# Running the stages of three token jobs at the same time in a four-layer decoder trunk on eight cores

## Chip, cores, metric

One Trainium2 chip, all 8 cores, one sequence of the prompt and 16 sample sequences on each; no core talks to another. The metric is the time of one execution in device microseconds, that of the slowest core. Executions come in two states: fast, and slow, where one die (cores 0 to 3 or 4 to 7) shows a lower granted TensorE clock and the time is some per cent longer. The kernel before took 3514 to 3523 us in the undisturbed runs of every round of experiments, so times of different rounds can be set side by side.

In the profile's lines PE is TensorE's matmuls, PEld its weight loads, DVE VectorE, ACT ScalarE and POOL GpSimd. SBUF is where the kernels keep their tiles, PSUM where their matmuls put their sums (the tile PS in the lines). A table load is an ACT_TABLE_LOAD in ACT's list: 289 of them in the trace of the kernel before, 1283 ns each.

## The reference, cut to what matters

Four layers. On a core each handles 2048 prompt tokens and 16 x 4 sample tokens, 2112 in all, with 1024 channels.

```python
h = layer_norm(x) * (1 + scale) + shift                # per-sequence modulation from c
a_x, a_z, b_cg, b_bg, b_x, b_z, g_a, g_b = split(h @ w_in)   # 8 x 1024 columns
# branch A: conv4 -> gates r, i (block diagonal) -> a = exp(c r ..), b = sqrt(1-a^2) i x -> scan over tokens
o_a = (scan(a, b) * silu(a_z)) @ w_a_out
# branch B: conv3 of (b_cg * b_x), gated
o_b = (b_bg * conv3 * silu(b_z)) @ w_b_out
out = (sigmoid(g_a) * o_a + sigmoid(g_b) * o_b) @ w_o
x   = layer_norm(ALPHA * x + gate * out) * ln_g + ln_b
```

Data is channel by token: 8 chunks of 128 channels on the partitions, tokens along the free dimension. Phase 1 is everything up to the two branch products, phase 2 the two output projections with their sigmoid gates, phase 3 `w_o` with the residual.

## The kernel before: the parts that matter

The 2048 tokens go in two passes of 1024, each through all four layers with X resident in SBUF, in tiles of 512; the 64 sample tokens ride along in the first pass as a thin third tile. A greedy scheduler orders each engine's list ahead of time, and the program has each list in that order, with the semaphores to wait for.

```python
def tiles_of(s):
    if s == 0:
        return [(0, 0, 512, "p"), (1, 512, 512, "p"), (2, 1024, 64, "s")]
    return [(0, 0, 512, "p"), (1, 512, 512, "p")]
...
for s in range(2):
    load_x(s)                                  # TensorE transposes
    ...
    for (n, c0, W, kind) in tiles_of(s):
        ln_in(0, n, c0, W, kind)
    for l in range(DEPTH):
        phase1(l, s)
        for gi, g in enumerate(groups_of(s)):  # two groups of tiles
            phase2(l, s, g, gi)
            phase3(l, s, g, gi)                # ends with ln_out(l) and ln_in(l + 1)
```

```python
# LayerNorm statistics: two ones-matmuls per chunk, 16 a tile
cp("dve", xr, X[:, c, c0:c0 + W], ...)
P.add("pe", lambda e, ...: e.matmul(ps1, ones, xr, start=(c == 0), stop=(c == NCH - 1)), ...)
act(sq, X[:, c, c0:c0 + W], AF.Square, ...)
P.add("pe", lambda e, ...: e.matmul(ps2, ones, sq, ...), ...)
...
act(TZ, az, AF.Tanh, ..., scale=0.5)                      # SiLU as tanh and a product
stt(TZ, TZ, 1.0, az, ALU.add, ALU.mult, ...)
...
act(A2, A2, AF.Sqrt, ..., bias=0.25, scale=-0.25)         # in phase 1, stage 2
```

Of the kernel before, what the change touches and what calls it, by code (L numbers as in the profile page):

```python
# [7 lines left out]
BF16 = mybir.dt.bfloat16  # L8
AF = mybir.ActivationFunctionType
ALU = mybir.AluOpType  # L10

D = 1024
# [5 lines left out]
ST = 4  # L18
ALPHA = (2.0 * DEPTH) ** 0.25
LN_EPS = 1e-6  # L20
UNITS_PER_LAYER = 45
TW = 1088

STAT_FP32R = True
CFG = dict(tslots=4, mulalt=True, groupwise=True, nwb=8, single_bx=False, ln_dedicated=False, lnr=4, window=100)

class Buf:
    __slots__ = ("name", "w", "rs", "const")

    def __init__(self, name):  # L30
        self.name = name
        self.w = None
        self.rs = []
        self.const = False

class Op:
    __slots__ = ("eng", "fn", "deps", "sem", "val", "inc", "cost", "lat", "tbl", "idx", "start", "finish", "dma")

ENGS = ("pe", "act", "dve", "pool", "sp")
SYNC_LAT = 0.25  # L40
TBL_SWITCH = 1.3
WINDOW = 48
SCHEDULE = True
PRIO_Q = 0.4

class Prog:
# [10 lines left out]
    def add(self, eng, fn, reads=(), writes=(), dma=None, cost=0.3, lat=0.0, tbl=0):  # L57
        deps = []
        for b in reads:
            if b.w is not None:  # L60
                deps.append(b.w)
        for b in writes:
            if b.w is not None:
                deps.append(b.w)
            deps.extend(b.rs)
        op = Op()
        op.eng = eng
        op.fn = fn
        op.cost = cost
        op.lat = lat  # L70
        op.tbl = tbl
        op.idx = self.nops
        self.nops += 1
        op.dma = dma
        op.start = None
        op.finish = None
        if dma is None:
            op.sem = self.esem[eng]
            op.val = None
            op.inc = 1  # L80
        else:
            if dma not in self.dsem:
                self.dsem[dma] = self.stack.enter_context(self.nc.semaphore("dsem_" + dma))
                self.dcnt[dma] = 0
            self.dcnt[dma] += 16
            op.sem = self.dsem[dma]
            op.val = self.dcnt[dma]
            op.inc = 16
        seen = set()
        dl = []  # L90
        for d in deps:
            if id(d) not in seen and d is not op:
                seen.add(id(d))
                dl.append(d)
        op.deps = dl
        for b in reads:
            if not b.const:
                b.rs.append(op)
        for b in writes:
            b.w = op  # L100
            b.rs = []
        self.q[eng].append(op)
        return op

    def schedule(self):
        pend = {e: list(self.q[e]) for e in ENGS}
        allops = sorted((o for e in ENGS for o in self.q[e]), key=lambda o: o.idx)
        bl = {}
        succ_max = {}
        for o in reversed(allops):  # L110
            b_ = o.cost + o.lat + succ_max.get(id(o), 0.0)
            bl[id(o)] = b_
            for d in o.deps:
                v = b_ + (0.0 if d.eng == o.eng else SYNC_LAT)
                if succ_max.get(id(d), 0.0) < v:
                    succ_max[id(d)] = v
        head = {e: 0 for e in ENGS}
        free = {e: 0.0 for e in ENGS}
        newq = {e: [] for e in ENGS}
        cur_tbl = 0  # L120
        remaining = sum(len(v) for v in pend.values())
        done = {e: [False] * len(pend[e]) for e in ENGS}
        while remaining:
            best = None
            for e in ENGS:
                lst = pend[e]
                n = len(lst)
                h = head[e]
                while h < n and done[e][h]:
                    h += 1  # L130
                head[e] = h
                cnt = 0
                i = h
                cand = None
                while i < n and cnt < CFG['window']:
                    if not done[e][i]:
                        cnt += 1
                        op = lst[i]
                        rdy = 0.0
                        ok = True  # L140
                        for d in op.deps:
                            if d.finish is None:
                                ok = False
                                break
                            t = d.finish if d.eng == e and d.dma is None else d.finish + SYNC_LAT
                            if t > rdy:
                                rdy = t
                        if ok:
                            st = rdy if rdy > free[e] else free[e]
                            sw = 1 if (e == "act" and op.tbl != 0 and op.tbl != cur_tbl) else 0  # L150
                            key = (round((st + (TBL_SWITCH if sw else 0.0)) / PRIO_Q), -bl[id(op)], op.idx)
                            if cand is None or key < cand[0]:
                                cand = (key, st, sw, i, op)
                    i += 1
                if cand is not None and (best is None or cand[0] < best[1][0]):
                    best = (e, cand)
            assert best is not None, "scheduler deadlock"
            e, (key, st, sw, i, op) = best
            if sw:
                st += TBL_SWITCH  # L160
                cur_tbl = op.tbl
            elif e == "act" and op.tbl != 0:
                cur_tbl = op.tbl
            op.start = st
            free[e] = st + op.cost
            op.finish = st + op.cost + op.lat
            done[e][i] = True
            newq[e].append(op)
            remaining -= 1
# [3 lines left out]
    def emit(self):  # L173
        nc = self.nc
        prog = self
# [7 lines left out]
        def run(ename, eng):  # L183
            waited = {}
            for op in prog.q[ename]:
                for d in op.deps:
                    if ename == "pe" and d.eng == "pe" and d.dma is None:
                        continue
# [4 lines left out]
                ins = op.fn(eng)  # L193
                ins.then_inc(op.sem, op.inc)
            if ename == "sp":
                for op in prog.finals:
# [5 lines left out]
        with nc.Block() as block:  # L202
# [19 lines left out]

def bc_last(ap, n):
    return bass.AP(ap.tensor, ap.offset, [list(x) for x in ap.ap] + [[0, n]])

# [5 lines left out]

def _build(nc, stack):
# [5 lines left out]
    xp_d = dram("xp", [SEQ, D], "ExternalInput")  # L238
    xs_d = dram("xs", [NSB * ST, D], "ExternalInput")
    sst_d = dram("sst", [DEPTH, 96, D], "ExternalInput")  # L240
    cvec_d = dram("cvec", [17, D], "ExternalInput")
    prm_d = dram("prm", [64, D], "ExternalInput")
    wmain_d = dram("wmain", [DEPTH * UNITS_PER_LAYER, 128, 2048], "ExternalInput")
    wc_d = dram("wc", [DEPTH * 12, 128, 2048], "ExternalInput")
    ident_d = dram("ident", [128, 128], "ExternalInput")
    yp_d = dram("yp", [SEQ, D], "ExternalOutput")
    ys_d = dram("ys", [NSB * ST, D], "ExternalOutput")
    pst_d = dram("psto", [DEPTH, 6, D], "ExternalOutput")
    sso_d = dram("sso", [DEPTH, 96, D], "ExternalOutput")
# [3 lines left out]

    X = sb("X", [128, NCH, TW])
    HN = sb("HN", [128, NCH, TW], BF16)
    YA = sb("YA", [128, NCH, TW], BF16)
    YB = sb("YB", [128, NCH, TW], BF16)
    MGW = 576 if CFG["groupwise"] else TW
    MG = sb("MG", [128, NCH, MGW], BF16)
    XB = [[Buf(f"X{c}_{n}") for n in range(3)] for c in range(NCH)]  # L260
    HNB = [[Buf(f"HN{c}_{n}") for n in range(3)] for c in range(NCH)]
    YAB = [[Buf(f"YA{c}_{n}") for n in range(3)] for c in range(NCH)]
    YBB = [[Buf(f"YB{c}_{n}") for n in range(3)] for c in range(NCH)]
    MGB = [[Buf(f"MG{c}_{n}") for n in range(3)] for c in range(NCH)]

    NWB = CFG['nwb']
    WB = [sb(f"WB{i}", [128, 2048], BF16) for i in range(NWB)]
    WBB = [Buf(f"WB{i}") for i in range(NWB)]
    WG = sb("WG", [128, 2048], BF16)
    WGB = Buf("WG")  # L270

    PRM = sb("PRM", [128, NCH, 64])
    PRMB = Buf("PRM")
    SST = sb("SST", [128, DEPTH, NCH, 96])
    SSTB = [[Buf(f"SST{l}_{c}") for c in range(NCH)] for l in range(DEPTH)]
    PST = sb("PST", [128, DEPTH, NCH, 6])
    PSTB = [[Buf(f"PST{l}_{c}") for c in range(NCH)] for l in range(DEPTH)]
    MOD = sb("MOD", [128, DEPTH, 24, 17])
    MODB = [Buf(f"MOD{l}") for l in range(DEPTH)]
    SCT = sb("SCT", [128, NCH, 17])  # L280
    SCTB = Buf("SCT")
    SH = sb("SH", [128, DEPTH, NCH])
    S1 = sb("S1", [128, DEPTH, NCH])
    HBR = sb("HBR", [128, DEPTH, NCH])
    HBI = sb("HBI", [128, DEPTH, NCH])
# [78 lines left out]
    for g_ in isgate:  # L364
        ngidx.append(cnt_)
        if not g_:
            cnt_ += 1
# [671 lines left out]
```

## Time and profile before

| | before |
|---|---|
| median of its first three runs | 3523 us (3516 to 3716, the highest one slow) |
| profiled run, cores | 3502 to 3531 us, granted clock 0.931 to 0.947 |
| TensorE busy | 86% of the span, but 72% by column count (worked out in the prediction) |
| DVE, ACT, POOL busy | 63%, 58%, 39% |
| 16 DMA engines, weight queue | 51.3% |

The way to read it: a matmul's recorded duration overlaps the next one's (512 columns: 379 ns recorded, 216 ns from start to start, medians of the trace), so the busy share of TensorE flatters it.

### The profile page before, as it was taken

The page shows a single profiled execution, that of the slowest core. Times are in us where ns is not written, and L with a number is a line of the kernel's source. Part 1 is how long each engine was busy: PE and PEld are TensorE (multiplying, and loading weights), DVE is VectorE, ACT ScalarE, POOL GpSimd, SP SyncE. Part 2 cuts the span into 40 slices and gives each one's busy share as a digit, 9 for nine tenths or more (in the row PEclk, how much of TensorE's full clock was granted, in tenths as well). Part 3 has the DMA queues.
Part 4 walks back from the last instruction along what each step waited for, and adds up shares of the span by engine and source line. Part 5 has one row for each costly group of instructions (what it writes and reads, how often), then busy time and mean ns, then how long its engine had stood idle before and what let it go on. Part 6 is the DMA issues. An engine that isn't in the chain of part 4 may idle for free.

```text
span 3531.2 us, 56621 instructions; the slowest of 8 cores (3502.1 to 3531.2 us)
## 1 busy us (share of the span) xinstructions
PE 3050.5 (86%) x15904; PEld 1455.2 (41%) x15904; DVE 2238.0 (63%) x3596; ACT 2048.9 (58%) x3386; POOL 1360.4 (39%) x1982
## 2 busy tenths in 40 slices
PE   5698997999978899788888698979999799979987
PEld 3344443444434444433445343434344344434444
DVE  1777457774567756577644587467846785568644
ACT  2677346774447754377633587348834784468623
POOL 1455223553225542245511265225532464235511
PEclk8899998998989999899998799999999899989998
DMA  7455943547544466523566334853387237724573
GB/s 151 66 90 90 142 73 61 88 80 122 89 72 76 79 109 104 95 37 55 83 122 120 88 65 81 134 96 60 67 143 120 42 67 121 131 48 72 93 131 87
DMA packets 88051, 322.39 MB, mean 91 GB/s; under 512 B 9817, under 2 KB 9945, under 8 KB 87746
## 3 DMA queue, kind: packets, MB, share of 16 engines
q0 software_dynamic: 81792, 297.83, 51.3%
q1 hardware_dynamic: 5954, 20.95, 1.8%
q8 instruction: 136, 2.23, 0.2%
q14 instruction: 169, 1.38, 0.1%
HBM read 606.21 MB, written 10.32 MB: 175 GB/s over the span
## 4 chain that ended last, share of the span: by engine, by line
PE 55%; ACT 13%; DVE 11%; issue 10%; POOL 6%; DMA 4%; DVEq 0%; ACTq 0%; POOLq 0%; SPq 0%
PE PS L455 50%; ACT TMPALL L417 9%; DVE TMPALL L441 4%; DVE TMPALL L430 4%; ACT L417 3%; POOL TMPALL L430 3%; PE PS L569 2%; PE PS L572 2%; DMA TMPALL<-xp 1%; DMA WB<-wmain 1%; DVE TMPALL L809 1%; POOL YA L430 1%; PE PS L461 1%; POOL PST L448 1%; POOL YB L430 1%
## 5 line engine op out<-in xcount | busy, mean ns | idle before, releaser
L455 PE MATMUL PS<-HN,WB 128*128 128x512 bf16 (+1 forms) x10240 | 1993.9, 350 | 232.3 <-ACT TMPALL L417 76.6
L455 PEld LDWEIGHTS PS<-HN,WB 128*128 128x128 bf16 x10240 | 866.8, 99 | 1255.8 <-issue 411.6
L417 ACT ACTIVATE TMPALL<-PS 128x512 f32<-128x512 f32 (+1 forms) x1052 | 530.3, 524 | 584.5 <-PE PS L455 433.3
L441 DVE SCALAR_TENSOR_TENSOR TMPALL<-TMPALL,PRM 128x512 f32<-128x512 f32 (+1 forms) x800 | 605.5, 767 | 141.9 <-ACT TMPALL L417 112.7
L441 DVE SCALAR_TENSOR_TENSOR TMPALL<-TMPALL,PS 128x512 f32<-128x512 f32 (+1 forms) x640 | 373.9, 588 | 487.4 <-PE PS L455 406.5
L383 POOL DMA_DIRECT2D WB<-wmain x512 | 288.0, 563 | 1019.2 <-PE PS L455 783.5
L430 POOL TENSOR_TENSOR TMPALL<-TMPALL 128x512 f32<-128x512 f32 (+1 forms) x288 | 380.0, 1328 | 516.9 <-ACT TMPALL L417 425.9
L417 ACT ACT_TABLE_LOAD x289 | 370.8, 1283 | 82.3 <-PE PS L455 28.0
L417 ACT ACTIVATE LNR<-X 128x512 fp32r<-128x512 f32 (+1 forms) x320 | 171.2, 551 | 333.1 <-PE PS L572 208.0
L417 ACT ACTIVATE TMPALL<-TMPALL,PRM 128x512 f32<-128x512 f32 (+1 forms) x320 | 219.2, 692 | 153.3 <-DVE TMPALL L430 103.4
L455 PE MATMUL PS<-MG,WB 128*128 128x512 bf16 (+1 forms) x1280 | 250.5, 353 | 51.8 <-DVE MG L430 27.3
L809 DVE TENSOR_TENSOR_SCAN TMPALL<-TMPALL,PST 128x512 f32<-128x512 f32 x128 | 205.0, 1604 | 88.7 <-POOL TMPALL L430 82.1
L455 PE MATMUL PS<-YA,WB 128*128 128x512 bf16 (+1 forms) x1280 | 259.6, 348 | 1.1 <-ACT TMPALL L417 1.1
L455 PE MATMUL PS<-YB,WB 128*128 128x512 bf16 (+1 forms) x1280 | 255.9, 345 | 2.0 <-DVE TMPALL L441 1.7
L430 DVE TENSOR_TENSOR TMPALL<-X,TMPALL 128x512 f32<-128x512 f32 (+1 forms) x320 | 221.8, 730 | 26.6 <-ACT TMPALL L417 22.7
L430 POOL TENSOR_TENSOR YB<-TMPALL 128x512 bf16<-128x512 f32 x160 | 201.9, 1262 | 80.0 <-DVE TMPALL L430 49.8
L430 POOL TENSOR_TENSOR YA<-TMPALL 128x512 bf16<-128x512 f32 (+1 forms) x160 | 197.2, 1233 | 74.5 <-DVE TMPALL L809 53.9
L430 DVE TENSOR_TENSOR TMPALL<-PS,TMPALL 128x512 f32<-128x512 f32 (+1 forms) x320 | 188.1, 591 | 53.0 <-PE PS L455 22.5
L448 POOL COPY PST<-TMPALL 128x3 f32<-128x3 f32 (+2 forms) x384 | 139.6, 366 | 182.3 <-ACT TMPALL L417 95.9
L455 PEld LDWEIGHTS PS<-MG,WB 128*128 128x128 bf16 x1280 | 109.3, 103 | 183.3 <-issue 84.8
L430 DVE TENSOR_TENSOR TMPALL<-TMPALL 128x512 f32<-128x512 f32 (+2 forms) x224 | 157.4, 727 | 43.1 <-ACT TMPALL L417 32.7
L569 PE MATMUL PS<-LNR,ONES 128*128 128x512 f32 (+1 forms) x320 | 140.8, 474 | 47.7 <-DVE LNR L448 46.2
(69 smaller groups left out, 2563.1 us busy)
## 6 DMA issues: line engine op xcount, KB each, us to landing
WB<-wmain POOLq DMA_DIRECT2D x512, 512.0 KB, 6.9
WB<-wc POOLq DMA_DIRECT2D x48, 512.0 KB, 9.9
TMPALL<-xp SPq DMA_DIRECT2D x16, 512.0 KB, 8.2
yp<-TMPALL SPq DMA_DIRECT2D x16, 512.0 KB
WG<-wmain POOLq DMA_DIRECT2D x8, 512.0 KB, 11.6
TMPALL<-sst SPq DMA_DIRECT2D x4, 384.0 KB, 4.2
sso<-TMPALL SPq DMA_DIRECT2D x4, 384.0 KB
TMPALL<-xs SPq DMA_DIRECT2D x1, 256.0 KB, 11.5
```

Of the source, the lines that this page charges most:

```text
L383: P.add("pool", lambda e, dst=dst, srcd=srcd: e.dma_start(out=dst[:, :], in_=srcd), writes=[dB], dma=tag, cost=0.65, lat=5.0)
L417: return P.add("act", lambda e: e.activation(out=out, in_=in_, func=func, **kw), reads, writes, cost=cost, tbl=TBL.get(func, 0))
L430: return P.add(eng, lambda e: e.tensor_tensor(out=out, in0=in0, in1=in1, op=op), reads, writes, cost=ew_cost(eng, out, True))
L441: return P.add("dve", lambda e: e.scalar_tensor_tensor(out=out, in0=in0, scalar=scalar, in1=in1, op0=op0, op1=op1), reads, writes, cost=ew ...
L448: return P.add(eng, lambda e: e.tensor_copy(out=out, in_=in_), reads, writes, cost=ew_cost(eng, out, False))
L455: ins = e.matmul(out, l_, r_, start=(i == 0), stop=(i == n - 1))
L461: return P.add("pe", lambda e: e.transpose(out, in_, ident), reads, writes, cost=0.12, lat=0.15)
L569: P.add("pe", lambda e, c=c, xr=xr: e.matmul(ps1, ones, xr, start=(c == 0), stop=(c == NCH - 1)), reads=[LNRB[qx], ONESB], writes=[BANKB[b ...
L572: P.add("pe", lambda e, c=c, sq=sq: e.matmul(ps2, ones, sq, start=(c == 0), stop=(c == NCH - 1)), reads=[LNRB[qs], ONESB], writes=[BANKB[b ...
L809: P.add("dve", lambda e: e.tensor_tensor_scan(out=HS, data0=A, data1=TI, initial=PST[:, l, c, 0:1], op0=ALU.mult, op1=ALU.add), [TMPB[qA], ...
```

## The change

The intent is to keep TensorE supplied at every moment, by running stages of different token groups at once. The 2112 tokens become three equal jobs of 704. In slot k, phase 1 of job k, phases 2 and 3 of job k-1, LayerNorm out of job k-2 and LayerNorm in of job k+1 are laid over one another; X lives in DRAM between uses. With it: SiLU as one ACT function, the square root as Ln and Exp, LayerNorm sums pre-added on DVE and POOL, PSUM pairs given out by the scheduler, and the host lays data out channel-major, so no transposes.

```diff
+NJOB = 3
+W = (SEQ + NSMP) // NJOB          # 704
+HW = W // 2                       # a matmul's columns, 352
+NSLOT = DEPTH * NJOB
+P23_FROM, P23_SPAN = 0.01, 0.73
 ... (cut)
-    for s in range(2):
-        load_x(s)
 ... (cut)
-        for l in range(DEPTH):
-            phase1(l, s)
-            for gi, g in enumerate(groups_of(s)):
-                phase2(l, s, g, gi)
-                phase3(l, s, g, gi)
+    for k in range(NSLOT + 2):
+        if k < NSLOT:
+            place(k, p1_events(k))
+        if 1 <= k <= NSLOT:
+            place(k, p23_events(k - 1))
 ... (cut)
+        if 2 <= k:
+            place(k, ln_out_events(k - 2, 0.01, 0.2))
+            if k + 1 < NSLOT:
+                place(k, ln_in_events(k + 1, 0.22, 0.3))
+        if 1 <= k <= NSLOT:
+            place(k, [(0.53, lambda k=k, c=c: fetch_x(k - 1, c), None) for c in range(NCH)])
 ... (cut)
-        act(TZ, az, AF.Tanh, [BANKB[ids[1]]], [TMPB[qTZ]], scale=0.5)
-        stt(TZ, TZ, 1.0, az, ALU.add, ALU.mult, ...)
+                act(halves(T(z)), ps(blk), AF.Silu, [blk], [TMPB[z]], psum=True)
-        act(A2, A2, AF.Sqrt, [TMPB[qA2]], [TMPB[qA2]], bias=0.25, scale=-0.25)
+                act(T(m), T(m), AF.Ln, [TMPB[m]], [TMPB[m]], bias=0.25, scale=-0.25)
+                act(T(m), T(m), AF.Exp, [TMPB[m]], [TMPB[m]], scale=0.5)
```

## The prediction

> **What bounds the kernel now.** I read the table of cores first (3502 to 3531 us, granted clock 0.931 to 0.947, dies alike: a fast run), then the page's busy shares and 40 slices, then the stretches by engine, then who waited for whom.
>
> ```profile
> PE 3050.5 (86%) x15904; PEld 1455.2 (41%) x15904; DVE 2238.0 (63%) x3596; ACT 2048.9 (58%) x3386; POOL 1360.4 (39%) x1982
> PE   5698997999978899788888698979999799979987
> PEclk8899998998989999899998799999999899989998
> ```
>
> TensorE is busiest, but 86% is not its load. The reference fixes that: per layer 512 weight blocks of 128x128 for the input projection, 16 for the gates and 3 x 64 for the three output projections, 720 blocks, each against 2112 tokens on a core, in 4 layers: 6.08 million columns. The spacing of matmuls I take from dense stretches:
>
> ```profile
> core 3: us, PE busy (x) PEld busy (x) DVE busy (x) ACT busy (x) POOL busy (x), PEclk, DMA share, GB/s
> 2030.00:2075.00 45.00, 45.00 (x210) 20.43 (x209) 40.62 (x45) 39.59 (x57) 29.19 (x38) 1.00 0.41 70
> 2957.00:3002.00 45.00, 45.00 (x210) 20.43 (x209) 13.77 (x20) 11.80 (x18) 9.07 (x15) 1.00 0.96 157
> 2207.00:2251.00 44.00, 42.26 (x197) 19.00 (x195) 13.66 (x21) 7.89 (x14) 7.73 (x14) 1.00 1.02 168
> ```
>
> 45 us / 210 = 214.3 ns per 512 columns, 1 ns over 512 columns at 2.4 GHz, so the load is 6.08 million / 2.4 GHz = 2534 us plus 1 ns a matmul: 72% of 3523 us. Some 990 us are lost. The first row is what the reader should keep: in the projection stage (phase 1) all five engines overlap, DVE at 90% and ACT at 88%, and TensorE still runs gapless; in the output stage (rows two and three) the vector engines idle and the DMA queues are full. Where the 990 us go:
>
> ```profile
> 44.00:132.00 88.00, 62.55 (x280) 37.31 (x280) 42.91 (x100) 39.35 (x77) 20.87 (x20) 0.66 0.56 99
> 530.00:618.00 88.00, 62.42 (x372) 32.27 (x371) 66.27 (x159) 59.84 (x117) 31.10 (x39) 0.81 0.37 61
> 1898.00:2030.00 132.00, 90.41 (x474) 54.42 (x472) 78.34 (x149) 68.85 (x119) 30.66 (x36) 0.75 0.44 101
> 2030.00:2207.00 177.00, 164.31 (x753) 72.74 (x752) 147.03 (x163) 143.61 (x205) 107.15 (x140) 1.00 0.43 73
> 132.00:397.00 265.00, 232.48 (x1425) 109.75 (x1424) 188.07 (x348) 191.78 (x345) 136.98 (x237) 0.99 0.56 87
> ```
>
> Here TensorE looks 70% busy in the prologue, at a layer boundary (LayerNorm out, then in, then the next layer) and between the two passes, at clocks of 0.66 to 0.81. Counting only bf16 columns by shape, slice by slice, TensorE does 0 to 25% of its possible work in the prologue (112 of 132 us lost), and 31 to 62 us are lost at each layer boundary, about 114 between the passes and 63 at the end: together some 580 us. The other 400 are thin: phase 1 of the first pass (last row), which drags 64-column tiles along, does about 0.81 of its possible columns; the second pass (fourth row) 753 x 214.3 / 177 us = 0.91.
>
> ```profile
> PE PS L455 <- ACT TMPALL L417: 92.5, 89, 6.9
> PE PS L455 <- DVE TMPALL L441: 66.4, 68, 3.3
> PE PS L455 <- ACT HN L417: 62.3, 5, 17.2
> PE PS L569 <- DVE LNR L448: 46.2, 37, 6.8
> PE PS L455 <- DMA WB<-wmain: 15.3, 7, 2.8
> ```
>
> These are TensorE's own waits: for PSUM to be read, for the LayerNorm chain (third and fourth), hardly for weights. So it is a latency problem at boundaries, not an engine at its limit.
>
> [...] all eight cores show 1.00 in most dense stretches for over 100 us, while core 3 alone has 0.81 from 775 to 925 us. [...] the conv step on 128x512 takes 0.74 us alone and up to 1.47 us, mean 1.07 in the fourth row's stretch. [...] the trace has 289 loads of 1283 ns.
>
> **The change part by part.** It is a rewrite: three jobs of 704 tokens (prompt and samples in one row), in 13 pipeline slots; slot k runs phase 1 of job k, phases 2 and 3 of job k-1, and the LayerNorms of job k-2 and k+1 at once. X lives in DRAM between uses.
>
> TensorE. 720 x 2 halves x 12 = 17280 matmuls of 352 columns: 146.7 + 1 to 2 ns = 148 ns, 2557 us. Weight loads don't bind: 64-column matmuls follow each other at some 30 to 45 ns, with a load each. LayerNorm sums now add on DVE and POOL first, so 16 statistics matmuls per 512-token tile become 4 per 704, 96 in all, about 25 us; modulation 768 tiny ones, about 25. All input and output transposes go (the host does the layout). About 2610 us at full clock, or 217 us per full slot (phase 1: 800 x 148 ns = 118; phases 2 and 3: 640 x 148 ns = 95; 4 for the rest). No time is removed here; the load stays.
>
> DVE per slot, scaling rows of the by-form groups to 704 columns with the 64- and 512-column durations (a PSUM product takes 219 ns at 64 and 684 at 512, 1.04 ns a column, so 0.88 us at 704; the LayerNorm subtraction 217 and 858, so 1.13). Phase 1: the fourth row gives 147/16 = 9.2 us per chunk of 512; Silu on ACT removes two operations of 0.68; times 1.36 for length: 10.7 us x 8 chunks = 85 us. Phases 2 and 3: (2 x 0.88 + 1.0 + 0.95) x 8 = 30. Two LayerNorms: 2 x (1.0 + 1.13 + 1.39) x 8 = 56. Samples about 8. Sum 179 us, 79% of a 227-us slot; the first row above shows 90% harmless.
>
> ACT: 18 operations per chunk (12 in phase 1, two gate Tanh, two squares, two normalising) of 0.76 (from PSUM: 216 ns at 64, 593 at 512) to 0.97 us (with scale and bias by partition) = 14.9, x 8 = 119; some 28 table loads (2 to 3 per chunk, sqrt now as Ln and Exp) x 1.28 = 36; statistics 8: 163 us, 72%. POOL: 5.5 tensor operations of 1.85, copies 2.8, weight issues 3.4 = 16 per chunk, x 8 = 130, 57%.
>
> DMA. 528 + 48 + 4 weight units against 568. The queue needed 51.3% x 3531 / 568 = 3.2 us each: 1850 us; X traffic of 78 MB at the 330 GB/s of the hardware queue (20.95 MB in 1.8% of the span) is 236 more: 2090 us, 73%, spread evenly. A unit serves 32 x 148 ns = 4.7 us of matmuls.
>
> Sum. Prologue about 55 us (8 modulation units 26 us beside X at 9, statistics, then 8 x 2.5 us of normalising) for 132. Slot 0 has phase 1 only and ACT is its limit: about 145. Slots 1 to 11: I choose a fill of 0.955, above the 0.91 of phase 1, since independent output blocks can fill its holes, below the gapless rows: 217 / 0.955 = 227, x 11 = 2499. Last phases 2 and 3: 100. Last LayerNorm and store: 32. Together 2831 us; 1% for spells of 0.81 on the slowest core (150 us at 0.81 costs 28 us): **2850 us**, 19% off.
>
> **The rivals.** (1) The clock limiter. [...] For it: core 3's spell, and one run of before in three at 3716 us. Against: 2030 to 2207 us has all engines loaded at 1.00. Fully throttled: 2610 / 0.81 + 250 = about 3470; a third of the time: 3040. (2) The in-order queues of DVE and ACT become the bound: 79% and 72% on average, with contention if POOL at 57% overlaps DVE more, and only four PSUM pairs. If the DVE's SBUF operations go as in their worst spells, 179 becomes about 220 us a slot and 11 slots take some 2650: 3000 in all. [...] (3) The single X buffer: LayerNorm out, LayerNorm in, reload, phase 3 run in series in each slot; their planned shares (0.20, 0.30, 0.08, 0.14) leave a quarter of a slot free; if DVE lags, slots stretch to 240: 2980. (4) DMA sets the pace: it needs 73%, and 1.02 was reached without TensorE waiting; I expect nothing.
>
> **Range and chances.** A perfect fill gives 11 x 217 + 332 = 2720; fill of 0.90 with some throttling 3050. Range 2710 to 3050. For a gain under 2% a slot would have to take 285 us, above every rival but full throttling. Faster 0.95, same 0.03, slower 0.02.
>
> **What would show it.** Right: bf16 columns at 0.93 to 0.98 of possible from about 200 us to 2650; no slices of low PEclk but at the ends; DVE near 75% of the span, ACT 65 to 70%, DMA over 65%; TensorE's waits for LayerNorm outputs gone. Wrong: a clock near 0.81 in mid-kernel (rival 1); TensorE waiting on ACT or DVE for PSUM for more than 15 us a slot (2); waits of phase 3 for X (3); waits for weights (4). A prologue over 80 us would make that term wrong.

## The result, and the profile after

The changed kernel takes 2866 us (median of 13 runs, 2846 to 3169), the kernel before 3563 us in the 15 runs made by then. The ratio of the fast runs is 0.811 (95% interval 0.809 to 0.814). Ratios here and below are the mean time of one kernel's fast runs over that of the other's of the same rounds, so not quite the ratio of the medians quoted. The profiled run, slowest core 2845 us:

```profile
PE 2658.9 (93%) x18144; PEld 1729.4 (61%) x18144; DVE 2091.2 (74%) x2329; ACT 1716.1 (60%) x2051; POOL 1495.1 (53%) x1818
PE   2889999999999999999999999999999999999995
PEclk9999999999999999999999999999999999999997
q0 software_dynamic: 83520, 304.12, 64.2%
q1 hardware_dynamic: 32688, 81.45, 8.9%
```

The row of 40 slices has no hole between the third and the last: the dips at layer boundaries are gone, and with them the low clock (0.985 on average against 0.94). DMA stands at 64.2 + 8.9 = 73%.

The same stretches as in the prediction's sum, cut where the gate matmuls and the phase 3 matmuls show that a slot begins and ends (columns: stretch, its length, busy time and count of each engine, clock, DMA share, GB/s):

```profile
211.00:2708.00 2497.00, 2421.15 (x16439) 1578.16 (x16437) 1855.27 (x2064) 1538.40 (x1833) 1343.74 (x1654) 0.99 0.74 136
62.00:211.00 149.00, 128.43 (x927) 81.02 (x928) 122.86 (x107) 106.61 (x128) 106.30 (x105) 0.97 0.83 150
0.00:62.00 62.00, 5.80 (x132) 4.85 (x132) 36.08 (x51) 22.32 (x34) 20.33 (x32) 1.00 0.99 194
2708.00:2815.00 107.00, 101.37 (x643) 64.41 (x644) 56.19 (x80) 35.09 (x43) 21.37 (x26) 0.95 0.59 123
```

From the top: slots 1 to 11, slot 0, the prologue, the last phases 2 and 3; the last LayerNorm has the remaining 30 us. A slot is 2497 / 11 = 227 us. From one matmul of 352 columns to the next it is 149.0 ns (median; at most 336 of them start within 50 us). With the 216.0 ns of 512 columns in the kernel before, that is (216.0 - 149.0) / 160 = 0.42 ns a column, which bears out the 2.4 GHz that the prediction counts with, and 2 to 3 ns a matmul besides. The 64-column matmuls of the kernel before, 29.0 ns from one to the next (median), give the same: (216.0 - 29.0) / 448 = 0.42.

TensorE's longest waits are now these (who waited for whom: total us, times, longest):

```profile
PE PS L391 <- ACT TMP L359: 41.5, 38, 2.4
PE PS L391 <- DVE LNR L368: 38.6, 5, 26.3
PE PS L391 <- DVE TMP L372: 24.0, 14, 4.7
PE PS L391 <- ACT HN L359: 13.7, 1, 13.7
```

The second and fourth hold waits of 26.3 and 13.7 us; TensorE's list in order of time shows both in the prologue. What is left elsewhere are short waits for PSUM.

An account of the loss, in TensorE time against the 2534 us of columns. Before: 990 us, of them 580 at boundaries and ends and 410 inside the streams. After: 2845 - 2534 = 311 us, of them 62 + 30 at the ends and 219 inside. So of 678 us won (3523 - 2845) some 490 come from the boundaries and ends and 190 from fuller streams. Not all of the 490 can be overlap. By the prediction's own parts, some 290 us were at layer boundaries, 114 at the change of passes and 112 + 63 at the ends. At the change of passes TensorE transposed X out and in (from 1930 to 1975 us in the trace), which the change has no more, and the ends, which nothing overlaps, shrank by 83 us. What counts as "inside" also holds the 2 to 3 ns a matmul, the modulation and the LayerNorm sums. Whether that account is right, and what filled the streams, the experiments are to say.

### The profile page after: what moved, and what is told of

The parts are those of the page before. It is cut to its first block, busy times and chain, and to the rows that moved or that the text cites. A ratio compares the mean times of both kernels' runs of the same rounds, so it can differ in the third digit from the quotient of the medians.

```text
span 2844.7 us, 53436 instructions; the slowest of 8 cores (2840.8 to 2844.7 us)
## 1 busy us (share of the span) xinstructions
PE 2658.9 (93%) x18144; PEld 1729.4 (61%) x18144; DVE 2091.2 (74%) x2329; ACT 1716.1 (60%) x2051; POOL 1495.1 (53%) x1818
## 3 DMA queue, kind: packets, MB, share of 16 engines
q0 software_dynamic: 83520, 304.12, 64.2%
## 4 chain that ended last, share of the span: by engine, by line
PE 66%; DVE 13%; issue 10%; ACT 9%; POOL 1%; DMA 0%; DVEq 0%; ACTq 0%; SPq 0%; POOLq 0%
PE PS L391 65%; ACT TMP L359 7%; DVE TMP L372 5%; DVE TMP L368 4%; ACT L359 2%; DVE X L372 1%; POOL TMP L368 1%; DVE TMP L569 1%; DMA X<-x 0%; ACT X L359 0%; DVE MG L368 0%; PE PS L761 0%; DVEq L205 0%; DVE X L368 0%; DVE LNR L368 0%
## 5 line engine op out<-in xcount | busy, mean ns | idle before, releaser
L391 PE MATMUL PS<-HN,WB 128*128 128x352 bf16 x12288 | 1919.7, 315 | 85.6 <-ACT TMP L359 34.7
L391 PEld LDWEIGHTS PS<-HN,WB 128*128 128x128 bf16 x12288 | 1202.8, 98 | 745.3 <-issue 108.3
L359 ACT ACTIVATE TMP<-PS 128x704 f32<-128x704 f32 x624 | 459.1, 753 | 347.4 <-PE PS L391 325.0
L372 DVE SCALAR_TENSOR_TENSOR TMP<-TMP,PRM 128x704 f32<-128x704 f32 (+1 forms) x480 | 518.1, 1079 | 170.0 <-ACT TMP L359 140.9
L368 POOL TENSOR_TENSOR TMP<-TMP 128x704 f32<-128x704 f32 x240 | 446.2, 1863 | 165.9 <-ACT TMP L359 158.1
L359 ACT ACTIVATE TMP<-TMP 128x704 f32<-128x704 f32 (+1 forms) x337 | 264.7, 788 | 32.5 <-DVE TMP L372 2.6
L391 PE MATMUL PS<-YA,WB 128*128 128x352 bf16 x1536 | 245.0, 313 | 4.7 <-ACT TMP L359 4.7
L391 PE MATMUL PS<-YB,WB 128*128 128x352 bf16 x1536 | 246.1, 314 | 2.1 <-ACT TMP L359 2.1
L391 PE MATMUL PS<-MG,WB 128*128 128x352 bf16 x1536 | 241.7, 314 | 2.6 <-DVE MG L368 2.6
L368 DVE TENSOR_TENSOR TMP<-X,TMP 128x704 f32<-128x704 f32 x192 | 192.9, 1005 | 30.7 <-ACT TMP L359 23.2
```

Of the source, the lines that this page charges most:

```text
L359: return P.add("act", lambda e: e.activation(out=res(out), in_=res(in_), func=func, **kw), reads, writes, cost=0.14 + 0.09 * nap + n * 0.0 ...
L368: return P.add(eng, lambda e: e.tensor_tensor(out=res(out), in0=res(in0), in1=res(in1), op=op), reads, writes, cost=cost, lat=0.05)
L372: return P.add("dve", lambda e: e.scalar_tensor_tensor(out=res(out), in0=res(in0), scalar=scalar, in1=res(in1), op0=op0, op1=op1), reads, ...
L391: ins = e.matmul(PS[blk.pair][:, t * 512:t * 512 + HW], w, mov(t), start=(i == 0), stop=(i == len(steps) - 1))
```

## The experiments

Theory: the gain comes from hiding the boundaries (LayerNorms, loads, stores) of one job under other jobs' matmuls. Rivals: (a) it comes from mixing the DVE-heavy phase 1 with the weight-heavy phases 2 and 3, so that neither regime binds; (b) it comes from cheaper operations; and, on what bounds the new kernel: (c) DVE, (d) DMA, or just the column count.

### One job after the other

```diff
-    for k in range(NSLOT + 2):
-        (phase 1 of k, phases 2 and 3 of k-1, LayerNorms of k-2 and k+1 in one slot)
+    for k in range(NSLOT):
+        if k:
+            place(k, [(0.0, lambda k=k, c=c: fetch_x(k, c), None) for c in range(NCH)])
+            place(k, ln_in_events(k, 0.01, 0.1))
+        place(k, squeeze(p1_events(k), 0.12, 0.45))
+        place(k, squeeze(p23_events(k), 0.58, 0.42))
+        place(k, ln_out_events(k, 0.92, 0.07))
```

> The changed kernel with the same operations, tiles and engines, but one job after the other: LayerNorm in, phase 1, phases 2 and 3, LayerNorm out of a job all end before the next job's X is loaded. If the gain comes from hiding one job's stages under another's matmuls, each of the 12 jobs takes about 130 us of phase 1, 107 of phases 2 and 3 (the last slot of the changed kernel) and some 85 of LayerNorm out, store, load and LayerNorm in with TensorE idle: 3860 us, 3600 to 3950, above the kernel before; TensorE busy under 75%, granted clock under 0.92. If the gain comes from cheaper operations, wide tiles and no transposes, which all stay, it stays under 3100 us.

3488 us, ratio to before 0.989 (0.981 to 0.996). With all operations, tiles and layouts of the change kept and only the overlap taken away, the kernel is back within about 1% of the old time. My size was off: shorter than 3600. The stretches of one job show why (boundary, phase 1, phases 2 and 3, next boundary; first the page's slices):

```profile
PE   3993995799499399479759939939966993992996
PEclk9996997899699699789979969969987996996998
```

```profile
286.00:345.00 59.00, 3.90 (x15) 2.05 (x14) 43.52 (x46) 30.16 (x35) 13.24 (x8) 0.54 0.43 116
345.00:470.00 125.00, 122.91 (x832) 79.18 (x830) 75.84 (x70) 89.49 (x105) 70.21 (x90) 0.98 0.62 105
470.00:571.00 101.00, 97.50 (x690) 63.83 (x688) 40.62 (x46) 25.41 (x32) 29.40 (x38) 1.00 0.72 118
571.00:631.00 60.00, 2.86 (x8) 1.60 (x8) 44.84 (x59) 28.22 (x33) 12.80 (x8) 0.53 0.39 112
```

A boundary costs some 60 us, not the 85 I had allowed. The eleven of them (57 to 63 us each in TensorE's list) are 664 us together, and 3488 - 2846 = 642: the difference to the changed kernel is the exposed boundaries. The streams themselves take 125 + 101 = 226 us a job here, as long as a slot of the overlapped kernel. So their fill does not come from overlap. The serial kernel's loss against 2534 us is 664 + 61 + 29 = 754 us at boundaries and ends and 3484 - 2534 - 754 = 196 inside the streams. The account above holds: about 190 to 210 us of the gain are in the streams with or without overlap; this kernel gives them back by longer boundaries than the old one had (the old one kept X in SBUF and overlapped one group's LayerNorm with the other's matmuls).

### The two regimes apart, the boundaries still hidden

```diff
         def pos(b):
-            return P23_FROM + (b + 0.5) / 40 * P23_SPAN
+            return 0.01 + (b + 0.5) / 32 * 0.36 if b < 32 else 0.56 + (b - 31.5) / 8 * 0.12
 ...
-                ev.append(((n + 0.5) / 48, f, u))
+                ev.append((0.38 + 0.61 * (n + 0.5) / 48, f, u))
```

> The changed kernel with LayerNorms and loads still hidden under other jobs, but in each slot phase 2 of job k-1 placed ahead of phase 1 of job k (phase 3 among phase 1), so that the two regimes are no longer mixed chunk by chunk. If hiding the boundaries is what matters, and no engine is at its limit even in phase 1 alone (DVE some 85 us of 118), the time stays within 2%: 2850 to 2900 us. If mixing the two regimes is what matters, phase 1 alone runs at the fill of slot 0 (149 us for 118) and a slot takes 245 to 255 us: 3050 to 3150 us.

2866 us in its two undisturbed runs (a third had 2895 at a clock of 0.967 on one die), +0.7% against 2846. TensorE's list confirms the order: in a slot the 8 blocks of phase 2 now stand together in some 70 us, ahead of the gates of phase 1. No hole opens in the page's slices:

```profile
PE   1789999999999999999999999999999999999995
PEclk9999999999999999999999999999999999999998
```

Rival (a) falls: mixing phase 2 with phase 1 is worth 0.7%. Phase 3, a fifth of these blocks, stayed mixed with phase 1 here; the serial run, where nothing of another job is mixed in and a job's streams take 226 us all the same, covers that.

### Silu undone, and DVE work added

```diff
-                act(halves(T(z)), ps(blk), AF.Silu, [blk], [TMPB[z]], psum=True)
+                act(halves(T(z)), ps(blk), AF.Tanh, [blk], [TMPB[z]], scale=0.5, psum=True)
+                stt(halves(T(z)), halves(T(z)), 1.0, ps(blk), ALU.add, ALU.mult, [TMPB[z], blk], [TMPB[z]])
```

(with the gate's factor halved in two places to keep the result).

> Silu undone: Tanh on ACT and a product on DVE from PSUM as before, 192 more DVE operations of about 0.88 us, 169 us, DVE from 74 to 80% of the span. If TensorE's column count sets the pace: within 1%, at most 2875 us. If DVE's in-order queue is the bound (rival 2 of the prediction): most of the 169 us appear, 2960 us or more.

2898 us: +52, between the two expectations. DVE rose by 2273.1 - 2091.2 = 182 us, so 29% of it appears in the time. The line of engines from this run's page, to be compared with the first line shown of the changed kernel:

```profile
PE 2674.6 (92%) x18144; PEld 1734.7 (60%) x18144; DVE 2273.1 (78%) x2521; ACT 1708.2 (59%) x2051; POOL 1510.0 (52%) x1818
```

And TensorE's longest wait in this run, which in the changed kernel (the third line of its waits above) was 24.0 us:

```profile
PE PS L391 <- DVE TMP L372: 81.1, 44, 4.0
```

TensorE waits 57 us more for DVE to read PSUM; the wait for ACT to read it falls from 41.5 to 22.0, so the two together grow by 38 of the 52 us. That could be DVE's load or only the longer life of a PSUM block that now waits for two readers. So the same amount of DVE work was added without PSUM:

```diff
                 act(halves(T(z)), ps(blk), AF.Silu, [blk], [TMPB[z]], psum=True)
+                stt(T(z), T(z), 0.0, T(z), ALU.mult, ALU.add, [TMPB[z]], [TMPB[z]])
```

> The changed kernel, Silu kept, with a further DVE operation in SBUF (z times 0 plus z) after each Silu: 192 operations of about 1 us, as much DVE work as the run with Tanh added, but no PSUM block is held by it. If the 52 us of the Tanh run came from its product holding a PSUM block until DVE gets to it: at most 2860 us. If they came from DVE's load as such: 2890 us or more.

2916 us. The cores of die 0 had 153 us at a clock of 0.81 early in the profiled run (mean 0.970). Those of die 1 had no such spell (mean 0.977 to 0.980) and took 2896 to 2905 us, +52 to +62 against the 2841 to 2845 of the changed kernel's cores, for 192 us more DVE work: 27 to 32%. The engines, and TensorE's longest wait, which in the changed kernel was 2.5 us:

```profile
PE 2697.2 (93%) x18144; PEld 1740.0 (60%) x18144; DVE 2283.3 (78%) x2521; ACT 1717.3 (59%) x2051; POOL 1546.7 (53%) x1818
PE PS L391 <- DVE TMP L368: 45.1, 19, 3.5
```

So the block that Silu reads need not be held for this loss. But "no PSUM block is held by it" was not quite so: the added operation stands between the second Silu and the product that reads the next projection's block (`f_bg`), and the wait that grew is one for DVE's products. Whether each added microsecond costs through the load of DVE's queue or through this longer chain is not separated; no run added DVE work outside the chain. With an average of 74% DVE is not the bound, but it isn't free either: about three tenths of the work added in phase 1 comes through.

### The new operations in the old structure

Silu in the kernel before, with the scheduler's bookkeeping of table loads adapted:

```diff
-        act(TZ, az, AF.Tanh, [BANKB[ids[1]]], [TMPB[qTZ]], scale=0.5)
-        stt(TZ, TZ, 1.0, az, ALU.add, ALU.mult, ...)
+        act(TZ, az, AF.Silu, [BANKB[ids[1]]], [TMPB[qTZ]])
```

> The kernel before, with Silu in place of Tanh and the DVE product (320 DVE operations fewer, some 190 us of 2238, the scheduler's table groups adapted). If the boundaries are what binds the kernel before: at most 2% faster, 3450 to 3530 us. If the cheaper operations are a main part of the gain: 5% or more faster, under 3350 us.

3627 us, ratio 1.028 (1.019 to 1.038: above 1, but wide): slower, against the expectation, although DVE lost 186 us. Then the square root as Ln and Exp as well:

```diff
-        act(A2, A2, AF.Sqrt, [TMPB[qA2]], [TMPB[qA2]], bias=0.25, scale=-0.25)
+        act(A2, A2, AF.Ln, [TMPB[qA2]], [TMPB[qA2]], bias=0.25, scale=-0.25)
+        act(A2, A2, AF.Exp, [TMPB[qA2]], [TMPB[qA2]], scale=0.5)
```

> The kernel before with Silu and with the square root as Ln and Exp, the set of operations of the changed kernel in the old structure. If the slowdown of the run with Silu alone came from table sets (310 loads against 289, TensorE waiting 217 us for ACT against 92): table loads under 250 and a time of 3430 to 3530 us, within 2% of before. If Silu itself is at fault: 3580 us or more. If the operations carry the gain: under 3350 us.

3614 us, ratio 1.028 again (1.026 to 1.030). The number of table loads fell to 275 (289 before, 310 with Silu alone) without a gain, so the count is not it. Its loads, from the page's groups (count, busy time, ns of one):

```profile
L417 ACT ACT_TABLE_LOAD x275 | 352.8, 1283 | 38.9 <-DVE TMPALL L441 25.5
```

Its longest wait of TensorE, to be set against 92.5 us of the same wait in the prediction's list:

```profile
PE PS L455 <- ACT TMPALL L417: 184.2, 133, 10.2
```

TensorE waits twice as long for ACT to read PSUM. The traces say more: of TensorE's waits of 0.2 us and more for any of ACT's readings of PSUM, 7 of 93 have a table load inside in the kernel before (9 of 95 us), 43 of 150 with Silu alone (111 of 224 us) and 34 of 142 with Ln and Exp too (96 of 188 us). These grew by 101 and 87 us, and the kernels by 109 and 96. So what changed is where the loads stand, not how many there are. Why they stand there stays open, since the scheduler's whole order moved too. What is shown is enough for rival (b): Silu, Ln and Exp by themselves do not speed the old structure, and the serial run, which keeps every cheaper operation (pre-added LayerNorm sums and no transposes too), is only 1% faster than before. What fills the streams in the change is then something of its structure that the serial kernel still has. The tiling is the likeliest part: there are no 64-column tiles, and the old pass that carried them ran at 0.81 of its columns against 0.91 for the pass without. But this was not isolated, and the LayerNorm sums, the allocation of PSUM pairs and the new list order changed with it: what share each has stays open.

### DMA added

First, every fourth weight unit copied once more to a junk buffer in DRAM as it is loaded:

```diff
                 self.loaded += 1
+                if n % 4 == 3:
+                    j = n // 4 % 4
+                    load("sp", junk_d[j], self.seq[n], [], [junkB[j]], f"junk{j}", 1 << 20)
```

> The changed kernel with every fourth weight unit also copied from DRAM to a junk DRAM buffer on the SP queue: 144 copies of 1 MB, about 3.2 us of all 16 engines each by the rate of the weight queue, 460 us, DMA share from 73 to about 88%. If DMA has slack: within 1%, at most 2875 us, TensorE's waits for weights under 30 us. If DMA paces the slots (rival 4): 2950 us or more.

3498 us. The test was badly made: the copies were tied to the issue of the loads but to none of the work, and the last of 144 began at 2625 us of 3525. The DMA slices of its page:

```profile
DMA  9999799989988996899897999899797776768673
```

TensorE's longest wait:

```profile
PE PS L393 <- DMA WB<-wmain: 402.0, 41, 28.7
```

It shows that TensorE waited 402.0 us for weights where most DMA slices stand at 8 or 9, not how much room there is. So the copies were tied to the output of a phase 1 chunk, which spreads them:

```diff
                 give("p1", y, z)
+                if True:                       # the other run: if c % 2 == 0
+                    load("sp", junk_d[c % 4], wmain_d[base + 3 * c], [YBB[s]], [junkB[c % 4]], f"junk{c % 4}", 0)
```

> The changed kernel with one extra 1 MB copy from DRAM to a junk DRAM buffer per phase-1 chunk, spread over slots 0 to 11 by waiting for that chunk's output (the earlier run had bunched 144 of them into the first 2000 us): 96 copies of about 3.5 us of all engines, DMA share from 73 to about 84%. If DMA has slack when it is spread: at most 2875 us. If it paces TensorE: 2950 us or more.

> Half the dose: 48 extra copies, one per two chunks, DMA share about 79%. If DMA has slack: at most 2860 us. If DMA paces: half of what the run with 96 lost.

With 48 copies 2847 us, no change; with 96, 2879 us, +1.1%, a hair over the limit I had set. The queue shares of the two (48 first, then 96):

```profile
q0 software_dynamic: 83520, 304.12, 66.6%
q1 hardware_dynamic: 34224, 131.78, 18.4%
```

```profile
q0 software_dynamic: 83520, 304.12, 70.4%
q1 hardware_dynamic: 35760, 182.12, 24.6%
```

66.6 + 18.4 = 85% is free, 70.4 + 24.6 = 95% costs 1%. The changed kernel's 73% is not its bound. My estimates of 79 and 84% were low: the hardware queue's share rose from 8.9 to 18.4% of 2845 us, 270 us of all 16 engines for 48 copies, 5.6 us each where I had taken the weight unit's 3.2.

### Two tries to go further

The changed kernel beside a prologue with the small derived constants moved behind the first LayerNorm and one semaphore source per modulation unit:

```diff
-    MODB = [bufs(3) for _ in range(2)]
+    MODB = [bufs(12) for _ in range(2)]
-    for l in range(DEPTH):
-        (derived constants)
+    place(-1, [(0.72, derive, None)])
```

> The changed kernel unaltered, beside the next run on the same chip: 2846 us in its fast runs, as before.

> The changed kernel with a shorter prologue: the derived constants (24 small DVE operations amid the LayerNorm sums of the first job) are moved behind the first LayerNorm, and the normalised chunks wait for their own modulation unit instead of all eight. TensorE's first projection matmul comes at 50 to 54 us instead of 62, nothing else changes: 2835 to 2839 us against 2846, 0.3%. If the prologue is bound by the X and weight transfers alone (98% DMA share in its first 50 us), it stays at 2846.

The unaltered one: 2845 to 2847 us in its undisturbed runs. The other: 2851 us at best; its undisturbed cores took 2842 to 2849 us, the original's 2841 to 2845. The first projection matmul came at 57.4 us instead of 61.0 on core 4, but the last gate of slot 0 at 214 us instead of 210. The first matmul now waits for the moved constants (of the 24 operations 8 are ACT's, not DVE's as the expectation has it); that they stand ahead of slot 0's own work and so delay it is likely, not shown. No gain.

Then, since DVE's load shows through, the merge addition of phase 2 was moved to POOL:

```diff
-                tt("dve", MG[:, j, :], T(a), T(t), ALU.add, ...)
+                tt("dve" if j == NCH - 1 else "pool", MG[:, j, :], T(a), T(t), ALU.add, ...)
```

> Try at a faster version: the merge addition of phase 2 (96 DVE operations of 1.23 us, 118 us in all) goes to POOL for seven of eight chunks, 104 us off DVE, some 155 us onto POOL (53 to 58%). If DVE's load costs TensorE about 52 us per 190 us added, as the two runs with extra DVE work showed, and this works backwards too, the time falls by some 28 us: 2810 to 2830 us. If POOL's slower operation holds the merge slots or POOL's queue delays weight loads and gate products: 2846 us or more.

Two of its fast runs had 2831 us, three 2851; the original, too, has fast runs of 2845 to 2847 and others of 2866, where part of a die is at 0.975. Like with like: all eight cores of the profiled run took 2826 to 2830 us at a clock of 0.982 to 0.988, against 2841 to 2845. That is 0.5% faster than the change, 15 us where some 28 were expected; the intervals of the ratios to before (0.809 against 0.810 and 0.811) are too wide to tell them apart. DVE fell by 28 us rather than 104, because its operations on SBUF became longer while POOL, busier by 160 us, worked beside them. Groups of the changed kernel (busy time, mean ns of one):

```profile
L368 DVE TENSOR_TENSOR TMP<-TMP 128x704 f32<-128x704 f32 x192 | 183.3, 956 | 58.9 <-ACT TMP L359 50.8 <-DVE SM L368 0.2 <-issue 0.2
L368 DVE TENSOR_TENSOR TMP<-PS,TMP 128x704 f32<-128x704 f32 x192 | 169.3, 884 | 147.2 <-PE PS L391 107.7 <-ACT TMP L359 39.1
```

The same two groups with the addition on POOL:

```profile
L368 DVE TENSOR_TENSOR TMP<-TMP 128x704 f32<-128x704 f32 x192 | 213.6, 1114 | 58.3 <-ACT TMP L359 49.8
L368 DVE TENSOR_TENSOR TMP<-PS,TMP 128x704 f32<-128x704 f32 x192 | 169.3, 884 | 156.6 <-PE PS L391 117.1 <-ACT TMP L359 39.2
```

The product of two SBUF inputs goes from 956 to 1114 ns, the one with a PSUM input stays at 884: DVE's product on SBUF lengthened beside a busier POOL (1654.8 us for 1495.1), as the conv step of the kernel before did, and that takes back much of what moving the addition gave. The page's line of engines for this run, and the wait that was 24.0 us in the changed kernel:

```profile
PE 2662.1 (94%) x18144; PEld 1731.2 (61%) x18144; DVE 2063.2 (73%) x2245; ACT 1717.0 (61%) x2051; POOL 1654.8 (58%) x1902
PE PS L391 <- DVE TMP L372: 7.0, 5, 2.4
```

The 15 us gained are over half of the 28 us that DVE lost, not three tenths, so the rate of the two runs with added work does not explain them. TensorE waits 17 us less for DVE's readings of PSUM: the additions no longer stand in DVE's list between these readings. That this is the cause is likely, not shown.

## Why the prediction was right, point by point

**The total.** 2850 us predicted, 2846 in undisturbed fast runs. The terms (predicted, measured): prologue 55, 62; slot 0 145, 149; slots 1 to 11 2499, 2497; last phases 100, 107; last LayerNorm 32, 30. The 19 us set aside for spells of 0.81 did not occur in the undisturbed runs and about paid for the terms that were short by 14, so a total within 4 us is partly luck. (The prediction calls these 19 us 1%, and gives 28 us for such spells; its sum uses neither.)

**The load.** 148 ns a matmul was 149.0, some 17 us in all. The prediction's 214.3 ns for 512 columns counted a matmul already under way among the 210; from start to start it is 216.0. That nothing of it goes away and only the holes do was right, as the serial run shows.

**The fill.** 217 of 227 us, 0.956 for 0.955. That figure was chosen and not derived, so this close a hit is luck. And the reason I gave, that independent output blocks fill phase 1's holes, was nearly empty: with the regimes apart the kernel loses only 0.7%, and phase 1 alone in the serial run takes 125 us for 118 plus its modulation units. The fill of 0.91 to 0.81 that I read from the old kernel was no property of phase 1 as such.

**Slot 0.** The size was right, the reason not: ACT was to be its limit, but ACT is busy for 106.6 of 149 us and DVE for 122.9. In the serial run the same first phase 1, without the next job's X and LayerNorm, takes 127 us (61 to 188 us in TensorE's list). So 22 of the 149 us come from these; that they act through DVE's queue is argued.

**The engines.** DVE 169 us a slot for 179, ACT 140 for 163 (18 table loads a slot, not 28; the prediction's own "2 to 3 per chunk" would be 16 to 24), POOL 122 for 130, DMA 73% for 73%. ACT's 60% of the span is below the 65 to 70% named as a sign of being right.

**Two readings of the old trace.** The spell of 0.81 was not on core 3 alone: cores 2 and 3 both had it, from 766 to 927 us, while cores 0 and 1 of the same die stood at 0.98 between 775 and 925 us. And the conv step's longest time in the fourth row's stretch is 2.30 us, not 1.47. It does lengthen beside POOL: with no POOL tensor operation or copy at the same time it never takes over 0.76 us in the whole trace.

**The rivals.** The clock: no core's record has a spell of 0.81 in the profiled run (means 0.983 to 0.985 with all cores dense), as read from the stretch with every engine loaded. In three fast runs of 13 some cores of one die stood at 0.970 to 0.980 (2864 to 2867 us), and the slow runs go up to 3169 us, 323 more; the kernel before went up to 3874, 356 more. In one slow run of the experiment with the regimes apart the four cores of one die had 0.814 to 0.819 and 3278 to 3286 us, the other die 0.982 to 0.985 and 2863 to 2867 us, with the same kernel on both. DVE's queue as the bound was half right: not the bound, but 27 to 32% of the work added in phase 1 comes through. X waits and weight waits: none seen beyond the prologue. DMA: nothing up to 85%.

## What to carry to other kernels

Count the columns (or whatever the busiest engine must do) and list where in time they are missing: here most of what was missing sat at stage boundaries where every engine was half idle, and laying another job's matmuls over them brought most of that back (the missing change of passes and the shorter ends have their part in it). Test such a story by taking away only the overlap: it also shows which part of the gain the new tiling brings by itself. An engine at 74% average is not free work: of what was added to DVE here 27 to 32% came through. And a function that saves one engine time can go with longer waits of another: with Silu in the old structure DVE lost 186 us, and the kernel took 2.8% longer.
